# A one-core mixer layer: its first block loaded and multiplied in halves, a dot product ahead of an addition, and one split ahead of a norm

## Chip, core and metric

The kernel runs on one core of a Trainium2 chip. The metric is the device time of one execution in microseconds (us). The engines are named as in the profile: PE (TensorE, with PEld for its weight loads), DVE (VectorE), ACT (ScalarE), POOL (GpSimd), and SP (SyncE), which issues the transfers.

## What is computed

One layer of a hybrid backbone: the reference, cut to what the first stage of the kernel works on, is

```python
x = x + sincos_2d(n_lat, 1024)                       # x: 1024 tokens x 1024 channels
mod_lat = silu(c) @ ada_w + ada_b                    # 3 x 1024: shift, scale, gate
sh, sc, gt = split(mod_lat, 3)
h = rms_norm(x, norm_g) * (1 + sc) + sh
z = h @ w_in                                         # 56 column blocks of 128
u_lru, z_lru, u_fft, z_fft, u_pool, z_pool, gates = split(z)
# three branches (RG-LRU scan, Fourier mixing, pooling), each gated by silu(z_*),
# projected, merged by sigmoid gates, multiplied by w_out, added to x, normed
```

The context tokens go through the same weights later and only serve the scan's first states.

## The kernel before

Everything is kept transposed: channels on the 128 partitions, tokens along the row. `x` is eight tiles `xt[k]` of 128x1024, a block of `w_in` is 128 channels by 8 k by 128 columns. Products are made of parts: every float32 operand is split into a rounded high part and a rest (`split`: the high part is an ACT cast, the low part a DVE subtraction), and three products (high high, low high, high low) are added in PSUM.

The first stage makes the eight blocks z0 to z7 of `z_lru` before and around the norm. The norm needs the sum of squares over all channels, so z0 to z5 are multiplied with `x` scaled per channel only (`xs`: high part `xh`, rest `xl`), and the result is multiplied with the tokens' `rstd` afterwards; the shift is put in as a bias. The scale per channel, `gsc`, is a dot product of a row of the ada weights with silu(c): `dot_scale(k, 0)` on DVE, from the tile `ada_t[8 + k]` and `sb[0]`.

Loop over k = 0 to 7 (the loop around `dot_scale(k, 0)` and `wave(k, chunk(k, FIRST), xs)` in the listing): `dot_scale`, `xs_hi` (ACT), the square of `xt[k]` (ACT), `add_pos(k + 1)` (the positional term, DVE), `squares_add` (DVE), `xs_lo` (DVE), every second k the split of the next weight chunk, then `wave(k, ...)`: 24 products of 512 columns on PE, four blocks (z0 to z3) by three parts by two halves of the tokens. A chunk `wc` holds two k of the four blocks. In wave 7 the blocks come one after another (z2, z0, z1, then the sum of squares `ss` through a product with ones, then z3); ACT copies z0 to z2 out of PSUM (`copy_out`), z3 is read by DVE. Two ACT logarithms and two exponentials make `rstd` (`rstd_part`). Then eight waves of 12 products make z4 and z5 from the same `xs` (weights `wz`, two whole blocks), and eight more make z6 and z7 from the normed `ht` (high part `hh`).

All four engines other than PE issue in exactly the order of the code in this stage (`manual_schedule`), as PE does in the whole kernel; an engine that waits holds up all that stands behind it. SP issues transfers in code order too; a load waits until its buffer is free and until the eighth transfer before it has landed. Ahead of the first wave stands `warm_up(16)`, 16 calls of a float32 product (two products each on PE) on a constant tile.

Of the kernel before, what the change touches and what calls it, by code (L numbers as in the profile page):

```python
# [10 lines left out]
ALU = mybir.AluOpType  # L11
# [4 lines left out]
NK = 8  # L16
# [8 lines left out]
B_ULRU, B_ZLRU, B_UF, B_ZF, B_UP, B_ZP, B_G = 0, 8, 16, 20, 24, 28, 32  # L25
# [3 lines left out]
def tile_hybrid_mixer(  # L29
# [26 lines left out]
    V, S, G, PE, SP = nc.vector, nc.scalar, nc.gpsimd, nc.tensor, nc.sync  # L56
# [11 lines left out]
    def f4(name, shape=(128, 1024), pool=None):  # L68
        return (pool or p4).tile(list(shape), F32, tag="t4", name=name)

    def f2(name, shape=(128, 512)):
        return p2.tile(list(shape), F32, tag="t2", name=name)

    def r4(name, shape=(128, 1024), pool=None):
        return (pool or p4).tile(list(shape), F32R, tag="t4", name=name)
# [4 lines left out]
    def acc(name):  # L80
        return pacc.tile([128, 1024], F32, tag="acc", name=name)
# [28 lines left out]
    def f(t):  # L110
        return t.bitcast(F32)

    def act(o, i, func=AF.Identity, **kw):
        S.activation(out=o, in_=i, func=func, **kw)  # L114

    def tt(o, a, b, op):
        V.tensor_tensor(o, a, b, op=op)  # L117

    def stt(o, a, s, b, op0, op1, **kw):
        V.scalar_tensor_tensor(o, a, s, b, op0=op0, op1=op1, **kw)  # L120
# [15 lines left out]
    class Weight:  # L136
        def __init__(self, name, src, shape=(128, NK, 128), pools=(praw, pwt, pwt)):
            self.name, self.shape, self.pools = name, shape, pools
            self.raw = f4(name + "_f", shape, pools[0])
            SP.dma_start(out=self.raw, in_=src)  # L140

        def mk(self):
            self.hi, self.lo = (r4(self.name + n, self.shape, p) for n, p in zip(("_h", "_l"), self.pools[1:]))
# [46 lines left out]
    def mm3(o, pairs, first=True, last=True):  # L190
        n = len(pairs)
        for i, (wh, wl, xh, xl) in enumerate(pairs):
# [5 lines left out]
    sml = const.tile([128, N_SMALL], F32, name="sml")  # L198
    pos = const.tile([128, 320], F32, name="pos")
# [6 lines left out]
    gsc, shc = ([[const.tile([128, 1], F32, name=f"{n}{v}_{k}") for k in range(NK)] for v in range(2)]  # L206
                for n in ("gsc", "shc"))
# [23 lines left out]
    def item(key):  # L231
        for pre, b in (("u", B_ULRU), ("z", B_ZLRU), ("UF", B_UF), ("ZF", B_ZF), ("UP", B_UP), ("ZP", B_ZP),
                       ("g", B_G), ("h", B_G + 8), ("i", B_G + 16)):
            if key[:-1] == pre:
                return key, in_block(b + int(key[-1])), KK
        n = int(key[-1])
        return key, {"pa": pa, "pb": pb, "pc": pc}[key[:-1]][n], KK
# [4 lines left out]
    with tc.manual_schedule(engines={ET.PE}):  # L242
# [17 lines left out]
        xt = [f4(f"x{k}") for k in range(NK)]  # L260
        sb = [f4("sb0"), None]
        ada_t, wt, cx = {}, {}, []
        H = [slice(0, HALF), slice(HALF, T)]

        def load_ada(n):
            ada_t[n] = f4(f"ada{n}")
            SP.dma_start(out=ada_t[n], in_=ada[n])
# [3 lines left out]
        chunks = []  # L271

        def load_chunk(c):
            chunks.append(Weight(f"wc{c}", w_in[B_ZLRU:B_ZLRU + 4, :, 2 * c:2 * c + 2, :].rearrange("b p k o -> p b k o"),
                                 (128, 4, 2, 128), CHUNK_POOLS[c]))

        CHUNK_POOLS = ((praw, pwt, pwt),) * 3 + ((praw, p4, p4),)

        def load_w(nm):
            wt[nm] = Weight("w" + nm, item(nm)[1], KK, (praw, p4, p4))  # L280

        SP.dma_start(out=sb[0], in_=cc[0:1, :].to_broadcast([128, 1024]))
        load_ada(8)
        for k in range(NK):
            SP.dma_start(out=xt[k], in_=xT[k])
            if k == 0:
                SP.dma_start(out=pos, in_=k_pos)
                SP.dma_start(out=sml, in_=small)
            else:
                load_ada(8 + k)  # L290
            if k in (0, 2, 4):
                load_chunk(k // 2)
        SP.dma_start(out=edge, in_=k_edge)

        def add_pos(k, eng=V):
            v = xt[k].rearrange("p (r c) -> p r c", c=64)
            if k < 4:
                e = pos[:, k * 16:(k + 1) * 16].unsqueeze(2).to_broadcast([128, 16, 64])
            else:
                e = pos[:, 64 + (k - 4) * 64:64 + (k - 3) * 64].unsqueeze(1).to_broadcast([128, 16, 64])  # L300
            eng.tensor_tensor(v, v, e, op=ALU.add)
# [6 lines left out]
        def warm_up(n):  # L308
            for _ in range(n):
                PE.matmul(out=pre_ps[:, 0:512], lhsT=warm[:, 0:128], rhs=warm, start=True, stop=True)  # L310


        def rstd_part(vs, pss):
            for v, ps in zip(vs, pss):
                act(v, ps, AF.Ln, scale=1.0 / D, bias=eps)
            for v in vs:
                act(v, v, AF.Exp, scale=-0.5)


        def dot(t, v, dst):  # L320
            stt(junk, t, 1.0, sb[v], ALU.mult, ALU.mult, accum_out=dst)

        def dot_scale(k, v):
            t = ada_t.pop(8 + k)
            g = gsc[v][k]
            dot(t, v, g)
            stt(g, g, b1[:, k:k + 1], sml[:, O_NG + k:O_NG + k + 1], ALU.add, ALU.mult)

        def dot_shift(k, v):
            s_ = shc[v][k]  # L330
            dot(ada_t.pop(k), v, s_)
            tt(s_, s_, sml[:, O_AB + k:O_AB + k + 1], ALU.add)


        xs = {}

        def xs_hi(k):
            xs[k] = r4(f"xh{k}"), r4(f"xl{k}")
            act(xs[k][0], xt[k], scale=gsc[0][k])

        def xs_lo(k):
            stt(xs[k][1], xt[k], gsc[0][k], f(xs[k][0]), ALU.mult, ALU.subtract)
# [11 lines left out]

        def wave(k, ws, src):
            for n in range(3):
                for nm, hi, lo in ws:
                    o = pacc_t[nm]
                    for h in range(2):
                        x = src[k][n == 2][:, H[h]]  # L360
                        PE.matmul(out=bank(o, h), lhsT=lo if n == 1 else hi, rhs=x,  # L361
                                  start=k == 0 and n == 0, stop=k == NK - 1 and n == 2)

        def chunk(k, names):
            w = chunks[k // 2]
            return [(nm, w.hi[:, b, k % 2, :], w.lo[:, b, k % 2, :]) for b, nm in enumerate(FIRST) if nm in names]
# [4 lines left out]
        def bank(o, h):  # L371
            return o[h] if isinstance(o, list) else o[:, H[h]]
# [22 lines left out]

        act(sb[0], sb[0], AF.Silu)
        V.tensor_scalar(b1, sml[:, O_AB + 8:O_AB + 16], 1.0, 0.0, op0=ALU.add, op1=ALU.add)
        warm_up(16)
        sqs, zv = None, {}
        pacc_t = {"z0": acc("z0"), "z1": acc("z1"), "z2": acc("z2"), "z3": acc("z3")}  # L400


        def copy_out(nm):
            zv[nm] = [f2(f"v{nm}_{h}") for h in range(2)]
            o = pacc_t.pop(nm)
            for h in range(2):
                S.copy(zv[nm][h], bank(o, h))
# [14 lines left out]
        def squares_add(k):  # L422
            if k:
                tt(sq[0], sq[0], sq[k], ALU.add)
                del sq[k]


        add_pos(0)
        for k in range(NK):
            dot_scale(k, 0)  # L430
            if k == 0:
                chunks[0].ready()
            xs_hi(k)
            sq[k] = f4(f"sq{k}")
            act(sq[k], xt[k], AF.Square)
            if k < NK - 1:
                add_pos(k + 1)
            if k:
                squares_add(k - 1)
            xs_lo(k)  # L440
            if k % 2 and k < NK - 1:
                chunks[k // 2 + 1].ready()
            if k == 0:
                load_chunk(3)
            if k == 3:
                load_w("z4")
            if k == 4:
                load_w("z5")
            if 1 < k < 6:
                load_ada(k - 2)  # L450
            if k < NK - 1:
                wave(k, chunk(k, FIRST), xs)
        act(rss[:, 0:1], eps, AF.Ln)
        wt["z4"].ready()
        wave(7, chunk(7, ["z2"]), xs)
        copy_out("z2")
        wave(7, chunk(7, ["z0"]), xs)
        wave(7, chunk(7, ["z1"]), xs)
        ps = acc("ss")
        ps = [ps[:, sl] for sl in H]  # L460
        squares_add(7)
        for h in range(2):
            PE.matmul(out=ps[h], lhsT=ones, rhs=sq[0][:, H[h]], start=True, stop=True)
        sq.clear()
        copy_out("z0")
        rstd_part([rstd[:, H[0]], rstd[:, H[1]]], ps)
        copy_out("z1")
        wave(7, chunk(7, ["z3"]), xs)
        dot_shift(0, 0)
        load_ada(4)  # L470
        dot_shift(1, 0)
        load_ada(5)
        wt["z5"].ready()
        dot_shift(2, 0)
        load_ada(6)
        dot_shift(3, 0)
# [907 lines left out]
```

## Time and profile before

| | us |
|---|---|
| median of 3 runs | 1002.89 (1002.65 to 1003.63) |
| the profiled execution | 1002.09 |
| its span, first to last instruction | 1000.3 |
| PE busy in it | 988.7 |
| DVE busy | 582.1 |
| ACT busy | 522.2 |

The profile shows one execution. Times in it count from the start of the span. A group of instructions bears the line of the code that recorded it, which can be that of a helper (L114 is `act`, L117 `tt`, L120 `stt`, L129 the cast and L134 the subtraction of `split`, L361 the product of `wave`); so tiles tell more than lines. Buffer numbers are left out of names: `xh` is any `xh` of the eight, told apart by their times. A bracket at the end of a row tells how long the engine was idle ahead of it and what released it.

### The profile page before, as it was taken

What the parts mean: (1) busy time and instruction counts of PE and PEld (TensorE: products, weight loads), DVE (VectorE), ACT (ScalarE), POOL (GpSimd) and SP (SyncE); (2) the same over time, 40 slices, a digit from 0 to 9 for tenths busy, and PEclk for the clock granted to TensorE, in tenths of its full rate; (3) what the DMA queues carried; (4) which work ended last, traced back from release to release, by engine and by line L of the source; (5) the groups of instructions that cost most, each with busy time, mean ns of one, the idle gap of its engine ahead of it and who ended that gap; (6) DMA issues with size and microseconds to landing.
All of it is one profiled execution on the core that took longest, in us unless ns stands there. A gap on an engine that the chain in (4) does not pass through costs nothing.

```text
span 1000.3 us, 11785 instructions
## 1 busy us (share of the span) xinstructions
PE 988.7 (99%) x4686; PEld 810.3 (81%) x4686; DVE 582.1 (58%) x746; ACT 522.2 (52%) x618; POOL 21.7 (2%) x22
## 2 busy tenths in 40 slices
PE   9989999999999999999999999999999999999997
PEld 5868788878788887888878888778888888888886
DVE  6959457538557485563845628256565674456063
ACT  4443464295793956939599394884332221213131
POOL 0000000000000000000000000000000000000341
PEclk9999999999999999999999999999999999999999
DMA  9532595131322222343243312357655785324272
GB/s 347 229 108 83 197 382 231 64 105 67 108 103 96 101 85 90 127 166 134 70 167 105 132 64 95 106 184 258 217 185 187 244 315 188 137 91 134 71 252 75
DMA packets 48838, 152.53 MB, mean 152 GB/s; under 512 B 6544, under 2 KB 10128, under 8 KB 48784
## 3 DMA queue, kind: packets, MB, share of 16 engines
q1 hardware_dynamic: 48640, 151.53, 43.0%
q8 instruction: 37, 0.61, 0.2%
q10 hardware_dynamic: 144, 0.26, 0.1%
q14 instruction: 17, 0.14, 0.0%
HBM read 114.01 MB, written 37.75 MB: 152 GB/s over the span
## 4 chain that ended last, share of the span: by engine, by line
PE 94%; ACT 4%; DMA 1%; DVE 0%; issue 0%; POOL 0%; DVEq 0%; SPq 0%; POOLq 0%
PE z L361 9%; PE pi L193 3%; PE pg L193 3%; PE o L195 3%; PE pi L195 3%; PE o L193 3%; PE o L194 3%; PE pi L194 3%; PE pg L194 3%; PE ppa L195 3%; PE ppa L193 3%; PE pu L195 3%; PE pg L195 3%; PE pu L194 3%; PE pu L193 3%; PE ppa L194 3%
## 5 line engine op out<-in xcount | busy, mean ns | idle before, releaser
L114 ACT ACT_TABLE_LOAD x74 | 94.9, 1283 | 2.0 <-PEq L1374 0.7
L117 DVE TENSOR_TENSOR i<-i,xc 128x1024 f32<-128x1024 f32 x16 | 19.0, 1223 | 58.9 <-ACT i L114 58.9
L194 PE MATMUL o<-wo_l,mh 128*128 128x512 f32 (+1 forms) x136 | 51.2, 377 | 0.0
L195 PE MATMUL o<-wo_h,mh 128*128 128x512 f32 (+1 forms) x136 | 51.2, 376 | 0.0
L193 PE MATMUL o<-wo_h,ml 128*128 128x512 f32 (+1 forms) x136 | 51.2, 376 | 0.0
L193 PE MATMUL pi<-hh,i_l 128*128 128x512 f32 x128 | 50.8, 397 | 0.0
L193 PE MATMUL ph<-hh,h_l 128*128 128x512 f32 x128 | 50.5, 395 | 0.2
L193 PE MATMUL pg<-hh,g_l 128*128 128x512 f32 x128 | 50.5, 394 | 0.0
L194 PE MATMUL pi<-hl,i_h 128*128 128x512 f32 x128 | 49.9, 390 | 0.0
L195 PE MATMUL ph<-hh,h_h 128*128 128x512 f32 x128 | 49.9, 390 | 0.0
L195 PE MATMUL pi<-hh,i_h 128*128 128x512 f32 x128 | 49.9, 390 | 0.0
L194 PE MATMUL ph<-hl,h_h 128*128 128x512 f32 x128 | 49.8, 389 | 0.0
L194 PE MATMUL pg<-hl,g_h 128*128 128x512 f32 x128 | 49.8, 389 | 0.0
L195 PE MATMUL pg<-hh,g_h 128*128 128x512 f32 x128 | 49.8, 389 | 0.0
L193 PE MATMUL pu<-hh,u_l 128*128 128x512 f32 x128 | 49.8, 389 | 0.0
L194 PE MATMUL pu<-hl,u_h 128*128 128x512 f32 x128 | 49.8, 389 | 0.0
L195 PE MATMUL pu<-hh,u_h 128*128 128x512 f32 x128 | 49.8, 389 | 0.0
L193 PE MATMUL ppa<-yh,pa_l 128*128 128x512 f32 x128 | 49.8, 389 | 0.0
L194 PE MATMUL ppa<-yl,pa_h 128*128 128x512 f32 x128 | 49.8, 389 | 0.0
L195 PE MATMUL ppa<-yh,pa_h 128*128 128x512 f32 x128 | 49.8, 389 | 0.0
L129 ACT CAST xh<-xc 128x1024 fp32r<-128x1024 f32 x8 | 8.4, 1054 | 75.1 <-DVE xc L120 52.8
L120 DVE SCALAR_TENSOR_TENSOR junk<-ada,sb 128x1024 bf16<-128x1024 f32 x32 | 39.0, 1219 | 13.5 <-DMA ada<-in_ada 13.5
(378 smaller groups left out, 2614.8 us busy)
## 6 DMA issues: line engine op xcount, KB each, us to landing
ada<-in_ada SPq DMA_DIRECT2D x32, 512.0 KB, 8.6
x<-in_xT SPq DMA_DIRECT2D x8, 512.0 KB, 10.0
u_f<-in_w_in SPq DMA_DIRECT2D x8, 512.0 KB, 4.0
i_f<-in_w_in SPq DMA_DIRECT2D x8, 512.0 KB, 4.5
k_i<-ei SPq DMA_DIRECT2D x8, 512.0 KB, 2.9
z<-k_z SPq DMA_DIRECT2D x8, 512.0 KB, 5.4
k_y<-z SPq DMA_DIRECT2D x8, 512.0 KB, 2.6
h_f<-in_w_in SPq DMA_DIRECT2D x8, 512.0 KB, 4.3
```

What stands on the lines that cost most here:

```text
L114: S.activation(out=o, in_=i, func=func, **kw)
L117: V.tensor_tensor(o, a, b, op=op)
L120: V.scalar_tensor_tensor(o, a, s, b, op0=op0, op1=op1, **kw)
L129: S.copy(hi, src)
L193: PE.matmul(out=o, lhsT=wl, rhs=xh, start=first and i == 0, stop=False)
L194: PE.matmul(out=o, lhsT=wh, rhs=xl, start=False, stop=False)
L195: PE.matmul(out=o, lhsT=wh, rhs=xh, start=False, stop=last and i == n - 1)
L361: PE.matmul(out=bank(o, h), lhsT=lo if n == 1 else hi, rhs=x, start=k == 0 and n == 0, stop=k == NK - 1 and n == 2)
```

## The change

Three things are changed in the first stage.

- The first block. `x0` and the first weight chunk are loaded in halves: tokens 0 to 511, the chunk's first k, the other tokens, the second k. The small tables (`sml`, `pos`) come ahead of them, and each ada tile is loaded ahead of its `x` tile instead of behind it. `first_block()` runs `dot_scale(0, 0)` in front of the addition of the positional term, and adds, scales and splits in halves. `wave(0, ...)` takes the first halves of the tokens of all blocks first. `warm_up` makes 7 calls instead of 16.
- The dot product stands in front of the addition for this first k; for the others the order in code stays.
- In wave 7 the split of z5's weights (`wt["z5"].ready()`) and two of the shift products (`dot_shift`) stand in front of z1's product and so of the norm; z0 and z1 are copied out directly behind their products.

```diff
-            SP.dma_start(out=self.raw, in_=src)
+            if src is not None:
+                SP.dma_start(out=self.raw, in_=src)
...
+        SP.dma_start(out=sml, in_=small)
         load_ada(8)
-        for k in range(NK):
+        SP.dma_start(out=pos, in_=k_pos)
+        w0 = Weight("wc0", None, (128, 4, 2, 128), CHUNK_POOLS[0])
+        for h in range(2):
+            SP.dma_start(out=xt[0][:, H[h]], in_=xT[0][:, H[h]])
+            SP.dma_start(out=w0.raw[:, :, h, :],
+                         in_=w_in[B_ZLRU:B_ZLRU + 4, :, h, :].rearrange("b p o -> p b o"))
+        chunks.append(w0)
+        for k in range(1, NK):
+            load_ada(8 + k)
             SP.dma_start(out=xt[k], in_=xT[k])
...
-                for nm, hi, lo in ws:
-                    o = pacc_t[nm]
-                    for h in range(2):
+                order = [(w, h) for w in ws for h in range(2)]
+                if k == 0 and n == 0:
+                    order.sort(key=lambda v: v[1])
...
-        warm_up(16)
+        warm_up(7)
...
-        add_pos(0)
+        def first_block():
+            w = chunks[0]
+            w.mk()
+            dot_scale(0, 0)
+            x, e = xt[0].rearrange("p (r c) -> p r c", c=64), pos[:, 0:16].unsqueeze(2).to_broadcast([128, 16, 64])
+            xs[0] = r4("xh0"), r4("xl0")
+            S.copy(w.hi[:, :, 0, :], w.raw[:, :, 0, :])
+            for h in range(2):
+                r = slice(8 * h, 8 * h + 8)
+                tt(x[:, r], x[:, r], e[:, r], ALU.add)
+                act(xs[0][0][:, H[h]], xt[0][:, H[h]], scale=gsc[0][0])
+            S.copy(w.hi[:, :, 1, :], w.raw[:, :, 1, :])
+            for r in range(2):
+                tt(w.lo[:, :, r, :], w.raw[:, :, r, :], f(w.hi[:, :, r, :]), ALU.subtract)
+                if not r:
+                    xs_lo(0)
+            w.raw = None
+
+        first_block()
...
         wt["z4"].ready()
+        squares_add(7)
         wave(7, chunk(7, ["z2"]), xs)
         copy_out("z2")
         wave(7, chunk(7, ["z0"]), xs)
+        copy_out("z0")
+        for k in range(2):
+            dot_shift(k, 0)
+        wt["z5"].ready()
         wave(7, chunk(7, ["z1"]), xs)
+        copy_out("z1")
...
-        squares_add(7)
...
-        copy_out("z0")
...
-        copy_out("z1")
         wave(7, chunk(7, ["z3"]), xs)
-        dot_shift(0, 0)
         load_ada(4)
-        dot_shift(1, 0)
         load_ada(5)
-        wt["z5"].ready()
```

What this does to the order of the built programs is seen at three places. On SP, the first transfers of the program, before (`in_cc` is silu's argument, `in_small` the table `sml`, `in_ada` the ada weights, `in_xT` the tiles of x, `in_w_in` the weights):

```order
L282 DMA sb_133<-in_cc 128x1024
L267 DMA ada_135<-in_ada 128x1024
L285 DMA x_125<-in_xT 128x1024
L287 DMA pos<-in_k_pos 128x320
L288 DMA sml<-in_small 128x124
L140 DMA wc_f<-in_w_in 128x4x256
L285 DMA x_126<-in_xT 128x1024
L267 DMA ada_143<-in_ada 128x1024
```

The same place now:

```order
L284 DMA sb_133<-in_cc 128x1024
L285 DMA sml<-in_small 128x124
L268 DMA ada_136<-in_ada 128x1024
L287 DMA pos<-in_k_pos 128x320
L290 DMA x_125<-in_xT 128x512
L291 DMA wc_f<-in_w_in 128x4x128
L290 DMA x_125<-in_xT 128x512
L291 DMA wc_f<-in_w_in 128x4x128
L268 DMA ada_144<-in_ada 128x1024
L296 DMA x_126<-in_xT 128x1024
```

The tables moved ahead of the first ada tile, the first x tile and the first chunk come in alternating halves, and the second ada tile stands ahead of the second x tile (`x_126`).

On DVE, the start of the program before (`pos` marks the additions, `ada` the dot products):

```order
L397 TENSOR_SCALAR sc_83<-sml_78 128x8
L301 TENSOR_TENSOR x0_125<-x0_125,pos_79 128x1024
L120 SCALAR_TENSOR_TENSOR junk_169,gsc0_0_84<-ada8_135,sb0_133 128x1024
L120 SCALAR_TENSOR_TENSOR gsc0_0_84<-gsc0_0_84,sc_83,sml_78 128x1
L134 TENSOR_TENSOR wc0_l_198<-wc0_f_140,wc0_h_197 128x1024
L301 TENSOR_TENSOR x1_126<-x1_126,pos_79 128x1024
L120 SCALAR_TENSOR_TENSOR xl0_202<-x0_125,gsc0_0_84,xh0_201 128x1024
L120 SCALAR_TENSOR_TENSOR junk_169,gsc0_1_85<-ada9_143,sb0_133 128x1024
```

The same place now:

```order
L404 TENSOR_SCALAR sc_83<-sml_78 128x8
L120 SCALAR_TENSOR_TENSOR junk_171,gsc0_0_84<-ada8_136,sb0_133 128x1024
L120 SCALAR_TENSOR_TENSOR gsc0_0_84<-gsc0_0_84,sc_83,sml_78 128x1
L117 TENSOR_TENSOR x0_125<-x0_125,pos_79 128x512 x2
L117 TENSOR_TENSOR wc0_l_188<-wc0_f_139,wc0_h_187 128x4x128
L120 SCALAR_TENSOR_TENSOR xl0_192<-x0_125,gsc0_0_84,xh0_191 128x1024
L117 TENSOR_TENSOR wc0_l_188<-wc0_f_139,wc0_h_187 128x4x128
L307 TENSOR_TENSOR x1_126<-x1_126,pos_79 128x1024
L120 SCALAR_TENSOR_TENSOR junk_171,gsc0_1_85<-ada9_144,sb0_133 128x1024
```

The first dot product moved ahead of the first addition, and the addition for `x1` now stands behind all of the first block's work.

On ACT, from the split of z4's weights to the first part of the normed input (`hh0`), before:

```order
L129 CAST wz4_h_471<-wz4_f_321 128x1024
L407 COPY vz2_0_481<-z2_192 128x512
L407 COPY vz2_1_482<-z2_192 128x512
L407 COPY vz0_0_501<-z0_190 128x512
L407 COPY vz0_1_502<-z0_190 128x512
L114 ACTIVATE rstd_168<-ss_497,eps_82 128x512 x2
L114 ACT_TABLE_LOAD
L114 ACTIVATE rstd_168<-rstd_168 128x512 x2
L407 COPY vz1_0_509<-z1_191 128x512
L407 COPY vz1_1_510<-z1_191 128x512
L129 CAST wz5_h_527<-wz5_f_359 128x1024
```

The same place now:

```order
L129 CAST wz4_h_468<-wz4_f_318 128x1024
L414 COPY vz2_0_479<-z2_185 128x512
L414 COPY vz2_1_480<-z2_185 128x512
L414 COPY vz0_0_489<-z0_183 128x512
L414 COPY vz0_1_490<-z0_183 128x512
L129 CAST wz5_h_497<-wz5_f_356 128x1024
L414 COPY vz1_0_507<-z1_184 128x512
L414 COPY vz1_1_508<-z1_184 128x512
L114 ACTIVATE rstd_170<-ss_511,eps_82 128x512 x2
L114 ACT_TABLE_LOAD
L114 ACTIVATE rstd_170<-rstd_170 128x512 x2
```

The cast of z5's weights and the copies of z1 moved from behind `rstd` to in front of it. On DVE the order of the additions of squares, the shift products and the splits of z4 and z5 is the same in both programs.

## Rows read from the trace of the kernel before

**Rows 1.** The page, busy us of each engine, share of span.

```profile
PE 988.7 (99%) x4686; PEld 810.3 (81%) x4686; DVE 582.1 (58%) x746; ACT 522.2 (52%) x618; POOL 21.7 (2%) x22
```

**Rows 2.** Waits of PE, whole span: who, for whom, us, times, longest.

```profile
PE z L361 <- ACT wz_h L129: 3.9, 1, 3.9
...
PE p L193 <- DVE al L134: 0.3, 1, 0.3
```

**Rows 3.** Table of stretches: length, busy us and count by engine, PEclk, DMA, GB/s.

```profile
66.70:69.80 3.10, 3.08 (x7) 2.49 (x8) 3.06 (x5) 0.00 (x0) 0.00 (x0) 0.51 0.00 0
```

**Rows 4.** Order of time, PE: start, us, operation, out<-in, count, idle before.

```profile
1.31 15.77 PE L310 MATMUL warm<-warm 128*128 128x512 f32 x32 [1.31 <-POOL warm L257]
...
16.52 2.41 PE L361 MATMUL z<-xh,wc_h 128*128 128x512 f32 x8
...
22.39 1.98 PE L361 MATMUL z<-xh,wc_h 128*128 128x512 f32 x8
...
55.03 0.62 PE L361 MATMUL z<-xh,wc_h 128*128 128x512 f32 x2
...
59.12 1.88 PE L463 MATMUL ss<-sq,ones 128*128 128x512 f32 x4
...
62.22 0.62 PE L361 MATMUL z<-xh,wz_h 128*128 128x512 f32 x2
...
89.58 1.07 PE L361 MATMUL z<-hh,wz_h 128*128 128x512 f32 x4
```

**Rows 5.** Order of time, ACT: `xh` of k = 2, then around the norm.

```profile
22.12 1.15 ACT L114 ACTIVATE xh<-x,gsc 128x1024 fp32r<-128x1024 f32 x1 [2.69 <-DVE gsc L120]
...
52.24 1.04 ACT L129 CAST wz_h<-wz_f 128x1024 fp32r<-128x1024 f32 x1
...
56.59 1.08 ACT L407 COPY vz<-z 128x512 f32<-128x512 f32 x2 [3.31 <-PE z L361]
...
61.03 1.26 ACT L114 ACTIVATE rstd<-ss,eps 128x512 f32<-128x512 f32 x2 [2.01 <-PE ss L463]
...
63.61 1.15 ACT L114 ACTIVATE rstd<-rstd 128x512 f32<-128x512 f32 x2
```

**Rows 6.** Order of time, SP: issues of `sml`, first chunk, x1.

```profile
2.59 0.56 SPq L288 DMA_DIRECT2D sml<-in_small  x1
3.19 0.62 SPq L140 DMA_DIRECT2D wc_f<-in_w_in  x1
3.86 0.61 SPq L285 DMA_DIRECT2D x<-in_xT  x1
```

**Rows 7.** Transfers issued at these three times: KB, us from issue to landing.

```profile
sml<-in_small SPq DMA_DIRECT2D x1, 62.0 KB, 6.2
...
wc_f<-in_w_in SPq DMA_DIRECT2D x1, 512.0 KB, 7.1
...
x<-in_xT SPq DMA_DIRECT2D x1, 512.0 KB, 7.7
```

**Rows 8.** Order of time, DVE: k = 1, then around the norm, z7's weights.

```profile
14.88 1.22 DVE L120 SCALAR_TENSOR_TENSOR junk<-ada,sb 128x1024 bf16<-128x1024 f32 x1
...
16.27 1.22 DVE L301 TENSOR_TENSOR x<-x,pos 128x1024 f32<-128x1024 f32 x1
...
54.45 1.22 DVE L117 TENSOR_TENSOR sq<-sq,sq 128x1024 f32<-128x1024 f32 x1
55.59 1.22 DVE L120 SCALAR_TENSOR_TENSOR junk<-ada,sb 128x1024 bf16<-128x1024 f32 x1
...
56.93 1.22 DVE L120 SCALAR_TENSOR_TENSOR junk<-ada,sb 128x1024 bf16<-128x1024 f32 x1
...
66.70 1.23 DVE L134 TENSOR_TENSOR wz_l<-wz_f,wz_h 128x1024 fp32r<-128x1024 f32 x1 [8.35 <-ACT wz_h L129]
...
70.81 1.28 DVE L117 TENSOR_TENSOR vz<-z,rstd 128x512 f32<-128x512 f32 x2
...
87.09 1.22 DVE L134 TENSOR_TENSOR wz_l<-wz_f,wz_h 128x1024 fp32r<-128x1024 f32 x1
```

More of the change, by code (lines that the diff above doesn't have):

```diff
@@ L282, in tile_hybrid_mixer @@
         SP.dma_start(out=sb[0], in_=cc[0:1, :].to_broadcast([128, 1024]))
+        SP.dma_start(out=sml, in_=small)
         load_ada(8)
-        for k in range(NK):
-            SP.dma_start(out=xt[k], in_=xT[k])
[L286 to L291, printed above, removed]
+        SP.dma_start(out=pos, in_=k_pos)
[7 more added lines that the diff above has]
+            load_ada(8 + k)
+            SP.dma_start(out=xt[k], in_=xT[k])
+            if k in (2, 4):
                 load_chunk(k // 2)
@@ L356, in wave @@
             for n in range(3):
-                for nm, hi, lo in ws:
-                    o = pacc_t[nm]
-                    for h in range(2):
-                        x = src[k][n == 2][:, H[h]]
-                        PE.matmul(out=bank(o, h), lhsT=lo if n == 1 else hi, rhs=x,
-                                  start=k == 0 and n == 0, stop=k == NK - 1 and n == 2)
+                order = [(w, h) for w in ws for h in range(2)]
+                if k == 0 and n == 0:
+                    order.sort(key=lambda v: v[1])
+                for (nm, hi, lo), h in order:
+                    x = src[k][n == 2][:, H[h]]
+                    PE.matmul(out=bank(pacc_t[nm], h), lhsT=lo if n == 1 else hi, rhs=x,
+                              start=k == 0 and n == 0, stop=k == NK - 1 and n == 2)
         def chunk(k, names):
@@ L425, in squares_add @@
                 del sq[k]
-        add_pos(0)
+        def first_block():
[16 more added lines that the diff above has]
+        first_block()
         for k in range(NK):
[L430 to L433, printed above, removed]
+            if k:
+                dot_scale(k, 0)
+                xs_hi(k)
             sq[k] = f4(f"sq{k}")
@@ L439, in tile_hybrid_mixer @@
                 squares_add(k - 1)
-            xs_lo(k)
+            if k:
+                xs_lo(k)
             if k % 2 and k < NK - 1:
```

## The prediction

> **What bounds the kernel now.** I read the page first: TensorE (PE) is busy for 988.7 of 1000.3 us [rows 1], so the time is its products plus what stands ahead of the first one, what it waits later, and what it does at a low clock. The waits of PE come next: from the first product on there is one long one, 3.9 us for `wz_h`, the high half of the sixth block's weights (z5), and one of 0.3 us far behind [rows 2]. The table of stretches adds to the long wait: behind it PE worked for 3.1 us at a granted clock of 0.51, so at 1.2 instead of 2.4 GHz [rows 3]. Then the order of time on PE: 16 warm-up calls (32 products) keep it until 16.5 us, and after that it runs without a hole through seven waves. A wave of 24 products takes (55.03 - 22.39) / 6 = 5.44 us, so a product takes 0.227 us and a wave of 12 takes 2.72 [rows 4]. Last I read DVE and ACT, which make the inputs of those waves. There the reader sees what the total hides: DVE's work for one k takes as long as a wave, and since PE starts late, `xh` of k = 2 is ready at 22.12 + 1.15 = 23.27 [rows 5] where PE wants it at about 27.8.
>
> So PE can't gain the whole 6 us between its possible start and 16.5. It overtakes DVE after about 4.5 us, and from there on only an earlier DVE helps.
>
> **The first block in halves.** What counts is the landing of x1, since DVE's chain goes on from there. Pieces land in the order of issue: `sml` at 2.59 + 6.2 = 8.79, the weight chunk at 3.19 + 7.1 = 10.29, x1 at 3.86 + 7.7 = 11.56 [rows 6, 7]. A 512 KB piece of x therefore takes 1.27 us of the queue, and a 512 KB chunk, whose rows in memory are 1 KB and not 4 KB, takes 1.50. With halves, rows of the chunk are 512 B. Quartering a row's length has cost 0.23 us; halving it again I put at 0.1 to 0.25 for both halves together, so one half takes about 0.85. Its bounds are 0.75 (half of a whole one; shorter rows give no reason for less) and 1.50 (as many rows as the whole chunk had). One ada tile now lands ahead of x1. So x1 lands at 11.56 + 1.27 + (2 x 0.85 - 1.50) = 13.0, and going back from there the second weight half lands at 10.5, the second x half at 9.6, the first weight half at 9.0.
>
> The Trainium skill, page "DMA: Bandwidth & Descriptors", section Bandwidth, speaks against this step: transfers are to be batched to 1 MiB or more, with 341 GB/s measured at 1 MB and 138 at 64 KB. The rows here show 512 KB in each 1.27 us, 413 GB/s, where pieces queue behind each other, so the trace doesn't agree for whole pieces; for halves no run here shows it yet. By 341 GB/s the four halves would take 3.1 us instead of my 3.0 and the sum would lose 0.1; what the rule would do at its worst is a rival below.
>
> DVE's and ACT's halves are cheap: two ACT copies of 128x512 take 1.08 us together [rows 5] and two DVE products of that size 1.28 [rows 8], against 1.04 and 1.22 for whole tiles. On ACT: cast of the first weight half 9.0 to 9.55, first half of `xh` to 10.15. There PE starts; its seven warm-up calls are 14 of 32 products and over by about 9. On DVE, the dot product goes first and hides under the landing of x0. The second addition ends at 10.3, the second half of `xh` at 10.95, `xl` at 12.25, the second low weight half at 12.9. The addition for x1 waits for its landing until 13.1, the dot product follows 1.14 later at 14.25, and the addition for x2 another 16.27 - 14.88 = 1.39 later, at 15.63. Before, it began at 16.27 [rows 8]. **DVE's chain so moves ahead by 0.64 us.** By the bounds of a weight half it is +0.75 (then DVE's own work is the limit, not x1) to -0.65.
>
> On PE: wave 0 from 10.15 to 15.6; wave 1 waits for `xh` of k = 1 until 16.9 and ends at 22.3; wave 2 waits for 23.27 - 0.64 = 22.65. Waves follow each other at 5.44, as DVE's k do, so wave 7 begins at 22.65 + 5 x 5.44 = 49.85 and PE stands at `ss` 59.12 - 55.03 = 4.09 later, at 53.95. `ss` needs the sum of squares, which DVE ends at 54.45 + 1.22 = 55.67 before and 55.03 now. **PE waits 1.1 us there, and `ss` begins at 55.1 instead of 59.12: 4.0 us gained.** This wait covers about 1 us of any mishap in the waves ahead of it.
>
> **The sixth block's split ahead of the norm.** DVE's order stays; ACT's changes. Wave z4/z5 begins 62.22 - 4.0 = 58.2. ACT ends `wz_h` of z4 at 53.28 - 0.64 = 52.65; then copies of z2 and z0 (1.08 each), the cast for z5 (1.04), ending at 55.85, and the copy of z1, to 56.9. Queued behind that is the logarithm for `rstd`, on which `ss` releases ACT 61.03 - 59.12 = 1.91 after its start, at 57.0: the moved cast costs it nothing, by 0.1 us. On DVE two shift products (56.93 - 55.59 = 1.34 each) fill the time from 54.95 to 57.65, then the low half for z5 ends at 58.85. PE reads it with the seventh product, at 58.2 + 6 x 0.227 = 59.55: 0.7 us to spare. **So the stall goes whole.** Eight waves take 21.76 us instead of 89.58 - 62.22 = 27.36: 5.6 gained, 3.9 of waiting and 1.7 of low clock.
>
> What is late next? `rstd` is ready at 57.0 + (63.61 + 1.15 - 61.03) = 60.75. DVE gets to the product for z3 at 57.65 + (70.81 - 66.70) = 61.75, so 9.05 earlier, and the transfers that SP holds back for DVE and PE there (ada 6 and 7, weights z6 and z7) move with it. The low weights of z7 are then ready at 87.09 + 1.22 - 9.05 = 79.25 [rows 8], and PE reads them at 58.2 + 21.76 + 1.36 = 81.3: 2 us to spare. Behind this stage both programs wait for the same things, so the rest moves as a whole.
>
> **The sum** is 4.0 + 5.6 = 9.6 us. The profiled execution took 1002.09 us (span 1000.3), which gives 992.5; the median of the runs, 1002.89, lies 0.8 above it and gives 993.3, which I predict.
>
> **Rivals.**
> 1. A new gap turns the clock down once, likeliest at `ss` (1.1 us idle). Price as after the old stall, 1.7 us: 995.0. Against it: 0.3 us of waiting at `p` left the clock alone [rows 2]; gaps between 0.3 and 3.9 the trace doesn't show. In waves 0 and 1 most of it would be hidden by the later waits. 8%.
> 2. Halves land no sooner than whole pieces did (1.27 and 1.50 each): x1 lands 2.6 us later than I take it, and DVE is 1.9 late instead of 0.64 early. All else kept, the time is 995.9. For it: a weight half has as many rows as a whole chunk. Against it: bytes set the pace of all pieces in [rows 6, 7]. This is the rule of "DMA: Bandwidth & Descriptors" in the Trainium skill at its worst. 7%.
> 3. The split for z5 does not do what it says: ACT or DVE come to it late, or z7's weights stall the next wave. If the whole 5.6 stays, 998.9. It needs an error of 2 us in the slack of 0.7 or 2. 6%.
> 4. Slower: the gap after seven warm-up calls (9 to 10.15) or the one before wave 1 drops the clock, and it stays at 1.2 GHz. A wave then takes 5.44 more, and 2.7 us of later waits hide the first half wave. The gain is gone and 2 us more when this lasts 2.6 waves; through all seven it gives 993.3 + 38.1 - 2.7 = 1028.7. Against it: after the old stall the low stretch lasted 3.1 us of dense work [rows 3]. 3%. That activity releases the clock is also what the Trainium skill says, "TensorE: Matmul & The Clock Gate", Part 1, and the trace agrees at 66.7.
>
> That nothing changes by more than 2 us either way needs 3 twice, or a piece of 4: 2%.
>
> **How the numbers follow.** My forecast has 74%. Its own bounds are 993.2 (a weight half of 0.75) and 994.6 (of 1.50). Below them I allow 1.2 us: the three runs of before lie 1.0 apart (1002.65 to 1003.63), and the first landings may come a little sooner in one run than in another. Above, the range goes 1 us on and takes rival 1 in. So 992.0 to 995.6; left out are 2, 3 and 4, and the 2% below: 18%. Faster by over 0.2% (2 us, about what a measurement tells from no change): 74 + 8 + 7 + 6 = 95%; within 2%; slower 3%.
>
> **What would show it.** Right: first z product near 10.2, `xh` of k = 2 begins near 21.5, wave 7 near 49.9, a wait of about 1 us at `ss` released by DVE's addition of squares, no wait for `wz_h`, a granted clock of 1.00 throughout, and the first z6 product near 80. Wrong: `ss` near 54 without a wait (DVE was earlier), x1 landing after 14, a clock under 1 before 60 us, or a wait in front of z5 or z7.

## The result, and the profile after

The changed kernel takes 992.49 us (median of 4 runs, 991.95 to 993.12), the kernel before 1002.77 beside it (1002.47 to 1003.63): a ratio of 0.9896, interval 0.9879 to 0.9913, so 10.3 us (8.7 to 12.1) less. The forecast was 993.3. The profiled execution took 992.99 us, its span is 991.1.

The page of the changed kernel, busy us of each engine, and its waits of PE (who, for whom, us, times, longest), beside [rows 1, 2]:

```profile
PE 980.3 (99%) x4668; PEld 805.6 (81%) x4668; DVE 582.2 (59%) x748; ACT 522.2 (53%) x620; POOL 21.8 (2%) x22
...
PE z L368 <- ACT xh L114: 2.3, 2, 1.4
PE warm L316 <- POOL warm L258: 1.3, 1, 1.3
PE ss L493 <- DVE sq L117: 0.9, 1, 0.9
```

The long wait for `wz_h` is gone. Three shorter ones stand earlier: two for `xh`, one at `ss`. The table of stretches (length, busy us and count by engine, PEclk, DMA, GB/s) shows the full clock in waves 1 to 7 and in the waves of z4 and z5, where [rows 3] had 0.51:

```profile
17.30:55.40 38.10, 37.31 (x162) 30.16 (x162) 35.10 (x42) 21.18 (x24) 0.00 (x0) 1.00 0.60 233
58.70:80.40 21.70, 21.70 (x97) 17.97 (x96) 21.13 (x40) 9.28 (x11) 0.00 (x0) 1.00 0.54 190
```

The order of time on PE in the changed kernel (start, us, operation, tiles, count, idle before), beside [rows 4]:

```profile
1.31 7.85 PE L316 MATMUL warm<-warm 128*128 128x512 f32 x14 [1.31 <-POOL warm L258]
10.57 2.17 PE L368 MATMUL z<-xh,wc_h 128*128 128x512 f32 x8 [1.42 <-ACT xh L114]
...
17.27 2.11 PE L368 MATMUL z<-xh,wc_h 128*128 128x512 f32 x8 [0.88 <-ACT xh L114]
...
23.00 2.12 PE L368 MATMUL z<-xh,wc_h 128*128 128x512 f32 x8
...
50.37 0.62 PE L368 MATMUL z<-xh,wc_h 128*128 128x512 f32 x2
...
55.47 1.95 PE L493 MATMUL ss<-sq,ones 128*128 128x512 f32 x4 [0.86 <-DVE sq L117]
...
58.65 1.07 PE L368 MATMUL z<-xh,wz_h 128*128 128x512 f32 x4
59.56 1.07 PE L368 MATMUL z<-xh,wz_l 128*128 128x512 f32 x4
```

PE starts 5.95 us sooner (10.57 against 16.52) but is only 3.65 ahead at `ss`, as it now waits for ACT and DVE. The waves of z4 and z5 take 80.41 - 58.65 = 21.76 us instead of 27.36, and the first z6 product stands at 80.41 instead of 89.58: 9.17 us ahead, as much as the span (9.2).

ACT and DVE around the norm in the changed kernel, beside [rows 5, 8]:

```profile
54.74 1.07 ACT L129 CAST wz_h<-wz_f 128x1024 fp32r<-128x1024 f32 x1
55.69 1.10 ACT L414 COPY vz<-z 128x512 f32<-128x512 f32 x2
57.46 1.27 ACT L114 ACTIVATE rstd<-ss,eps 128x512 f32<-128x512 f32 x2 [0.67 <-PE ss L493]
...
13.40 1.22 DVE L307 TENSOR_TENSOR x<-x,pos 128x1024 f32<-128x1024 f32 x1
...
15.98 1.22 DVE L307 TENSOR_TENSOR x<-x,pos 128x1024 f32<-128x1024 f32 x1
...
52.96 1.22 DVE L134 TENSOR_TENSOR wz_l<-wz_f,wz_h 128x1024 fp32r<-128x1024 f32 x1 [2.10 <-ACT wz_h L129]
54.11 1.22 DVE L117 TENSOR_TENSOR sq<-sq,sq 128x1024 f32<-128x1024 f32 x1
...
57.92 1.23 DVE L134 TENSOR_TENSOR wz_l<-wz_f,wz_h 128x1024 fp32r<-128x1024 f32 x1
...
78.88 1.22 DVE L134 TENSOR_TENSOR wz_l<-wz_f,wz_h 128x1024 fp32r<-128x1024 f32 x1
```

z5's low weights are done at 57.92 + 1.23 = 59.15. PE reads them with the third of the four products that begin at 59.56, so at 60.0 (a product takes 0.227 us). ACT still idles 0.67 us ahead of the logarithm: the cast moved in front of it costs it nothing. z7's low weights are ready at 80.10 and read at about 81.8.

### The profile page after: what moved, and what is told of

Read it like the earlier page. It is cut to its first block, busy times and chain, and to the rows that moved or that the text cites. A ratio compares the mean times of both kernels' runs of the same rounds, so it can differ in the third digit from the quotient of the medians.

```text
span 991.1 us, 11759 instructions
## 1 busy us (share of the span) xinstructions
PE 980.3 (99%) x4668; PEld 805.6 (81%) x4668; DVE 582.2 (59%) x748; ACT 522.2 (53%) x620; POOL 21.8 (2%) x22
## 3 DMA queue, kind: packets, MB, share of 16 engines
q1 hardware_dynamic: 49312, 151.53, 43.1%
## 4 chain that ended last, share of the span: by engine, by line
PE 89%; ACT 4%; DVE 2%; DMA 1%; issue 0%; DVEq 0%; SPq 0%
PE z L368 5%; PE pi L194 3%; PE pg L194 3%; PE o L195 3%; PE o L196 3%; PE pi L196 3%; PE pg L196 3%; PE o L194 3%; PE pi L195 3%; PE ppa L196 3%; PE ppa L195 3%; PE pu L194 3%; PE pg L195 3%; PE pu L196 3%; PE pu L195 3%; PE ppa L194 3%
```

## Experiments

Landings differ from execution to execution: the addition of `pos` to x2 begins between 15.78 and 16.45 us in programs that load alike. So the table gives for each kernel the median of its runs and, from the order of time on PE in one profiled execution, the first z product, `ss`, the distance between them, and the first z6 product.

| kernel | median us | first z | ss | distance | z6 |
|---|---|---|---|---|---|
| before | 1002.77 | 16.52 | 59.12 | 42.60 | 89.58 |
| changed | 992.49 | 10.57 | 55.47 | 44.90 | 80.41 |
| again | 992.30 | 10.37 | 55.28 | 44.91 | 80.24 |
| part_a | 998.99 | 10.40 | 55.30 | 44.90 | 86.27 |
| part_b | 997.28 | 16.58 | 59.20 | 42.62 | 84.08 |
| warm11 | 999.01 | 12.46 | 55.55 | 43.09 | 86.28 |
| simple | 993.33 | 12.72 | 55.79 | 43.07 | 80.71 |
| gap3 | 993.33 | 11.02 | 55.93 | 44.91 | 80.87 |
| tables | 992.17 | 10.32 | 55.22 | 44.90 | 80.16 |
| gsq | 1000.83 | 10.71 | 63.37 | 52.66 | 88.33 |
| swap | 992.49 | 10.99 | 55.34 | 44.35 | 80.31 |
| sqfirst | 991.77 | 10.59 | 54.51 | 43.92 | 79.40 |
| gsq7 | 991.58 | 10.86 | 54.82 | 43.96 | 79.71 |
| best | 991.00 | 10.27 | 53.83 | 43.56 | 78.72 |

**The whole change again, and each part alone.** `again` is the changed kernel; `part_a` has the first block in halves and 7 warm-up calls, without the new order around the norm; `part_b` has that order alone:

```diff
         wt["z4"].ready()
+        squares_add(7)
...
+        copy_out("z0")
+        for k in range(2):
+            dot_shift(k, 0)
+        wt["z5"].ready()
```

> The changed kernel once more, beside the parts, with more rounds. Its profile put the gain at 9.2 us (the first z6 product at 80.41 instead of 89.58), the medians put it at 10.3. Theory 1 (the gain lies all ahead of z6 and the medians' surplus is run-to-run spread): 9.2 to 9.6 us faster. Theory 2 (something behind the first stage moved as well, so that the profiled execution shows too little): 10 to 10.5 us faster.

> The first block in halves, seven warm-up calls and the new order of the first transfers, with the order around the norm as before. Theory 1 (DVE's chain sets when the sum of squares is ready, and the old stall follows the norm): ss at 55.5, a wait of about 4 us for z5's high weights with a low clock behind it, 3.6 us faster than before. Theory 2 (an earlier start of PE counts by itself): 16.5 - 10.6 = 5.9 us faster.

> Only the order around the norm is changed: z5's split ahead of it. Theory 1: the wait of 3.9 us and the low clock behind it go whole, 5.6 us faster, and with the other part the gains add up to 9.2. Theory 2 (part of the stall comes back at z5's low weights or at z7's): less than 5, and the parts don't add up.

Measured: `again` 0.9898 [0.9883, 0.9913], 10.5 us; `part_a` 0.9961 [0.9948, 0.9973], 3.8 us; `part_b` 0.9946 [0.9934, 0.9959], 5.5 us. In the profiles `part_a` is 3.3 us ahead at z6 and `part_b` 5.5; together 8.8, the whole change 9.2 to 9.3. (By the medians `again` gained what its second theory expected, by the marks what the first did. From z6 to the end of the span its profile takes 990.5 - 80.24 = 910.3 us, the kernel before 910.7, where PE waits for `al` [rows 2]. But the changed kernel's own profile takes 910.7 as well (its weight loads wait 0.35 for the same `al`), so this half microsecond differs between executions of one program and isn't shown to be the change's.) Waits of PE, `part_a`:

```profile
PE z L368 <- ACT wz_h L129: 4.1, 1, 4.1
PE z L368 <- ACT xh L114: 1.6, 2, 0.9
PE warm L316 <- POOL warm L258: 1.3, 1, 1.3
PE ss L488 <- DVE sq L117: 0.9, 1, 0.9
```

and its stretch behind the first of them:

```profile
63.60:67.00 3.40, 3.40 (x10) 2.63 (x9) 3.30 (x9) 0.00 (x0) 0.00 (x0) 0.50 0.21 48
```

The stall of 4 us and the low clock behind it belong to the order around the norm alone, and the 5.6 us of that step is confirmed. In the profiles the parts add up to the whole within half a microsecond; the medians leave 1.0 to 1.2, which their intervals (1.2 us each way) cover.

**Is it the halves, or only fewer warm-up calls?** `warm11` is the kernel before with one number changed, and `simple` is `part_b` with the same number:

```diff
-        warm_up(16)
+        warm_up(11)
```

> The kernel before with 11 warm-up calls instead of 16 and nothing else: PE is free at about 12.6, when the whole first block is ready (12.7). Theory 1 (what held PE were the warm-up calls, and what holds it now is DVE's chain, so halves bring only the 0.3 us by which DVE's chain is earlier): ss at 55.8, 3.3 us faster than before, all but 0.3 of what the whole first part brings. Theory 2 (the halves' earlier start matters): about 2 us less than the first part, so 1.5 us faster.

> The kernel before with 11 warm-up calls and the order around the norm, but with x0 and the first weights whole and in the old order of loads. T1 (halves bring nothing beyond the earlier start of PE): ss near 55.5 as with 11 warm-up calls alone, no stall for the sixth block's weights, first z6 product near 80.5, and the time within 0.5 us of the changed kernel: 992.3 to 992.8. T2 (the halves move DVE's chain by the 0.64 us of the prediction): ss near 55.9, z6 near 81.0, 993.0 to 993.6.

`warm11` measured 0.9964 [0.9952, 0.9977], 3.75 us, as much as `part_a`, and at z6 both stand 3.3 us ahead. PE's first z product follows the warm-up calls at 12.46 without a wait; at `ss` PE waits for the same addition of squares as the changed kernel:

```profile
PE z L361 <- ACT wz_h L129: 3.9, 1, 3.9
PE warm L310 <- POOL warm L257: 1.3, 1, 1.3
PE ss L463 <- DVE sq L117: 0.4, 1, 0.4
```

`simple` measured 0.9907 [0.9893, 0.9920], 9.5 us. At z6 it stands 0.3 to 0.5 us behind the changed kernel, by the medians 0.8 to 1.0. So warm-up calls had held PE up, and cutting five of them gives nearly all of the first part. The halves let PE start 2.1 us sooner still, but the distance to `ss` grows from 43.1 to 44.9 in return; 0.3 to 0.5 us is left in the profiles. The medians would allow twice that, and which of the two holds is open. Whatever it is, it belongs to the halves, the new order of loads and the dot product's place together; no run parts them.

**What does a low clock in wave 0 cost?** `gap3` is the changed kernel with 3 warm-up calls:

```diff
-        warm_up(7)
+        warm_up(3)
```

> The changed kernel with 3 warm-up calls (6 products) instead of 7, so that PE stands idle from about 5 to 10.4 us. T1 (the waits ahead of wave 1, wave 2 and ss, 0.88 + 0.41 + 0.86 us in the changed kernel, are a reserve that hides what a low clock in wave 0 costs): a stretch at the low clock of about 3.4 us, as behind the old 3.9 us stall, makes wave 0 about 1.7 us longer; wave 1 then begins near 18.0 instead of 17.27, the waits shrink, ss begins within 0.3 us of 55.4, and the time is 992.3 within 0.5. T2 (the low clock is paid in full, or lasts): ss near 57 or later, 994.0 or more.

Measured: 0.9906 [0.9892, 0.9919], 9.5 us. The order of time on PE and DVE, and the table of stretches:

```profile
1.31 5.11 PE L316 MATMUL warm<-warm 128*128 128x512 f32 x6 [1.31 <-POOL warm L258]
11.02 3.78 PE L368 MATMUL z<-xh,wc_h 128*128 128x512 f32 x8 [4.60 <-ACT xh L114]
14.60 2.73 PE L368 MATMUL z<-xh,wc_l 128*128 128x512 f32 x8
...
19.01 1.98 PE L368 MATMUL z<-xh,wc_h 128*128 128x512 f32 x8
...
51.65 0.62 PE L368 MATMUL z<-xh,wc_h 128*128 128x512 f32 x2
...
54.56 1.22 DVE L117 TENSOR_TENSOR sq<-sq,sq 128x1024 f32<-128x1024 f32 x1
...
55.93 1.96 PE L493 MATMUL ss<-sq,ones 128*128 128x512 f32 x4
...
9.40:16.10 6.70, 5.08 (x12) 4.06 (x13) 5.91 (x7) 3.44 (x5) 0.00 (x0) 0.50 1.05 391
16.20:55.00 38.80, 38.80 (x172) 32.10 (x172) 35.73 (x45) 21.37 (x23) 0.00 (x0) 1.00 0.64 246
```

Behind 4.6 us of idle time the clock is at 0.50 until 16.1, and wave 0 takes 19.01 - 11.02 = 7.99 us instead of 17.27 - 0.88 - 10.57 = 5.82, so some 2.2 more. Yet `ss` stands 44.91 behind the first product, as in the changed kernel, because the waits shrink. By the marks, wave 0 and the wait behind it take 7.99 for 6.70, 1.29 more; from wave 7 to `ss` it is 55.93 - 51.65 = 4.28 for 55.47 - 50.37 = 5.10, 0.82 less; and waves 1 and 2, which PE now runs without a wait, make up the rest. (The 0.41 that was expected there is idle time of PE's weight loads for `xh`, not of its products.) Here too `ss` comes 0.15 behind DVE's addition of squares (54.56 + 1.22 = 55.78), so the reserve was just enough. `ss` came 0.5 later than was expected, with the first z product 0.45 late: this execution's first ada tile landed that much later. The median, 993.33, is 0.8 to 1.0 above the changed kernel's and outside the range of the first theory; the intervals cover that. So the marks of one profile show that waits on the way to `ss` are a reserve; that the low clock costs nothing in the median is not shown.

**Does sml in front cost anything?** `tables` moves the small table behind the first ada tile:

```diff
-        SP.dma_start(out=sml, in_=small)
         load_ada(8)
+        SP.dma_start(out=sml, in_=small)
```

> The changed kernel with sml (the small table) issued behind the first ada tile instead of ahead of it, so that the first ada tile and what follows it land about 0.3 us earlier. T1 (x1's landing, 13.38 in the changed kernel, sets DVE's chain): x1 lands near 13.1, ss begins 0.3 earlier (55.1) and the time is 0.3 lower, 992.0. T2 (x1's landing is set by all the bytes ahead of it, whatever their order, or DVE's own work in the first block is the limit): no movement within 0.1 us.

Measured: 0.9896 [0.9881, 0.9911], 992.17. `ss` begins 0.25 sooner than in the changed kernel and 0.06 sooner than in `again`. That agrees with a cost of up to 0.3 us, but is no more than executions differ. The other profiles point the same way: x1 lands at 13.13 here and at 13.09 in `best`, where the small table stands behind, and at 13.18 to 13.84 in the eight profiles with halves where it stands ahead. The size stays open.

**Is DVE's chain the bound, and can POOL relieve it?** `gsq` gives POOL six of the seven additions of squares, `gsq7` only the last one:

```diff
-                tt(sq[0], sq[0], sq[k], ALU.add)
+                (V if k == 7 else G).tensor_tensor(sq[0], sq[0], sq[k], op=ALU.add)
```

(in `gsq7` the other way round: G for k = 7.)

> The changed kernel with the additions of squares of k = 1 to 6 on POOL (GpSimd), the last one still on DVE. T1 (DVE's chain sets when ss may begin: 0.86 us of waiting for the addition of squares): DVE gets 1.14 us shorter for each k from k = 2 on, PE runs from wave 2 (23.0) without a wait, ss begins at 54.5 instead of 55.4 and the time is 0.9 lower, 991.4. POOL needs about 2.6 us for one addition (two halves of 1.30 in the program's rows on POOL) of 5.44 for each k. T2 (POOL's additions slow DVE's own, since both read the same memory): DVE's operations of 1.22 get longer while POOL works, ss begins at 55.4 or later, time 992.3 or more.

> The changed kernel with only the last addition of squares on POOL. It tells why the six additions on POOL cost 8.5 us. T1 (POOL and DVE exclude each other: whoever has begun an operation on two tensors holds the other up until it ends, as DVE's 1.22 became 2.74 and 3.42 there): POOL's 2.5 us fall into DVE's idle time from 50.9 on, DVE's split of z4's weights is held up until about 53.4 and ends 0.4 to 0.5 later than in the changed kernel, ss begins without a wait at 54.6, time 0.86 lower: 991.5. T2 (POOL as such is late or its release is slow): ss later than 55.4, time 992.3 or more.

`gsq` measured 1000.83, 0.998 [0.9971, 0.9988]: 8.3 to 8.5 us are lost of 10.3. DVE and POOL in the order of time:

```profile
18.39 2.55 POOL L431 TENSOR_TENSOR sq<-sq,sq 128x1024 f32<-128x1024 f32 x1 [16.99 <-ACT sq L114]
25.70 2.47 POOL L431 TENSOR_TENSOR sq<-sq,sq 128x1024 f32<-128x1024 f32 x1 [4.76 <-ACT sq L114]
...
19.28 2.74 DVE L134 TENSOR_TENSOR wc_l<-wc_f,wc_h 128x1024 fp32r<-128x1024 f32 x1 [0.61 <-ACT wc_h L129]
...
25.84 3.42 DVE L120 SCALAR_TENSOR_TENSOR junk<-ada,sb 128x1024 bf16<-128x1024 f32 x1
```

The dot product that begins at 25.84, while POOL's addition runs (25.70 to 28.17), ends at 29.26: 1.1 after POOL's, nearly its whole own length. So does the split: it ends at 22.02, and POOL's addition at 20.94. In both DVE stands still until POOL is done: it loses 1.5 and 2.2 us in two k where it saves 2 x 1.14. It also idles 0.61 ahead of each split, waiting for ACT or for the weights; in the changed kernel the additions fill this time for k = 3 and 5. That makes 2.0 of the 2.5 us by which two k got longer (38.00 - 24.65 = 13.35 between waves 2 and 4 for 2 x 5.44); the other 0.5 is not accounted for. This is the rule of the Trainium skill, "SBUF — State Buffer", section "Who interferes with whom", that DVE and GpSimd share one port pair and that it is an exclusive lock; the trace agrees, with 2.74 and 3.42 us for 1.22. In `gsq7` the one addition falls into DVE's idle time:

```profile
50.87 2.55 POOL L431 TENSOR_TENSOR sq<-sq,sq 128x1024 f32<-128x1024 f32 x1 [49.47 <-ACT sq L114]
...
53.28 1.23 DVE L134 TENSOR_TENSOR wz_l<-wz_f,wz_h 128x1024 fp32r<-128x1024 f32 x1 [2.12 <-ACT wz_h L129]
```

and the time is 991.58, 0.9886 [0.9869, 0.9902]. The distance from first z to `ss` is 0.94 shorter than in the changed kernel: the wait at `ss` is gone. DVE's split was not held up, against what was expected, since it waited for ACT's cast until POOL was as good as done.

**The same by order alone.** `sqfirst` puts the last addition of squares in front of z4's split on DVE, `swap` the cast of the second chunk in front of the square of x1 on ACT, and `best` has both and the order of loads of `tables`:

```diff
-        wt["z4"].ready()
         squares_add(7)
+        wt["z4"].ready()
```

```diff
-            act(sq[k], xt[k], AF.Square)
+            if k != 1:
+                act(sq[k], xt[k], AF.Square)
...
                 chunks[k // 2 + 1].ready()
+            if k == 1:
+                act(sq[k], xt[k], AF.Square)
```

> The changed kernel with the last addition of squares in front of the split of z4's weights on DVE, where DVE stands idle for 2.1 us (from 50.87) waiting for ACT's cast. T1 (the wait of 0.86 us at ss is only this one addition's place in DVE's order): the addition ends near 52.1, z4's low weights stay where they are, ss begins behind z1's last product at 54.6 without a wait and the time is 0.86 lower than the changed kernel's: 991.5. T2 (something else is late next: rstd, since ACT's copies end near 56.8, or z5's low weights): ss earlier, but z6 gains less than 0.5.

> The changed kernel with ACT's cast of the second weight chunk in front of its square of x1, so that DVE's 0.6 us of idle time at 19 us goes. T1 (DVE's chain sets both the wait ahead of wave 2 and the one at ss): the addition for x3 and all of DVE's later work move 0.6 ahead, the wait ahead of wave 2 (0.41) goes, ss still waits for DVE and begins 0.6 earlier (near 54.8), and the time is 0.6 lower: 991.8. T2 (the transfers of x3 or of its ada tile, which land at 15.96 and 14.66, or PE bound the chain there): less than 0.2.

> The changed kernel with three more changes together: the last addition of squares in front of z4's split, the cast of the second chunk in front of the square of x1, and sml issued behind the first ada tile. T1: 0.86 for the wait at ss, 0.41 for the wait ahead of wave 2 and 0.25 for the earlier landings: ss near 54.0, first z6 product near 78.9, 990.8. T2 (rstd or the weights of z6 and z7 are late next and take it back): 991.5 or more, with a new wait of PE between ss and z6.

`sqfirst`: 991.77, 0.9889 [0.9875, 0.9904]. DVE in the order of time, and PE at `ss`:

```profile
50.82 1.22 DVE L117 TENSOR_TENSOR sq<-sq,sq 128x1024 f32<-128x1024 f32 x1
53.02 1.23 DVE L134 TENSOR_TENSOR wz_l<-wz_f,wz_h 128x1024 fp32r<-128x1024 f32 x1 [0.98 <-ACT wz_h L129]
...
54.51 1.88 PE L493 MATMUL ss<-sq,ones 128*128 128x512 f32 x4
```

No wait is left at `ss`, and z6 stands 0.8 to 1.0 ahead of the changed kernel's two profiles. `swap`: the distance is 0.55 shorter, as its first theory says, but the median is 992.49, no lower: in its profile the first ada tile landed at 7.70 instead of 7.25, and whether that took the gain in the other runs too is open. `best`: 991.00 (990.62 to 991.49), 0.9882 [0.9867, 0.9897], the lowest median of all; z6 is at 78.72, 1.7 ahead of the changed kernel's. In its profile 0.4 us of that is lost again at `p`, where PE waits for DVE's `al` as it did for 0.3 us in [rows 2]. The intervals of `best` and of the changed kernel overlap; that it is faster rests on the marks and on run ranges (990.62 to 991.49 against 991.95 to 993.12) that don't touch, though the two were not measured side by side (the kernel before took 1002.62 beside `best` and 1002.77 beside the changed kernel).

## Why the prediction held, point by point

- **PE's start and what it gives back.** First z was put at 10.15 and came at 10.57; wave 1 at 16.9, came at 17.27; `xh` of k = 2 near 21.5, came at 21.79; wave 2 at 22.65, came at 23.00. PE does overtake DVE there, and `warm11` and `simple` show that a start earlier than 12.5 us brings no more than half a microsecond in the profiles.
- **Landings.** Of the terms, a weight half was right: put at 0.85, with bounds 0.75 and 1.50, and measured at 0.8 from the issues and the times to landing (here the first ada tile, the first weight half and x1):

```profile
1.65 0.42 SPq L268 DMA_DIRECT2D ada<-in_ada  x1
...
3.06 0.43 SPq L291 DMA_DIRECT2D wc_f<-in_w_in  x1
...
5.80 0.45 SPq L296 DMA_DIRECT2D x<-in_xT  x1
...
ada<-in_ada SPq DMA_DIRECT2D x1, 512.0 KB, 5.6
...
wc_f<-in_w_in SPq DMA_DIRECT2D x1, 256.0 KB, 6.2
...
x<-in_xT SPq DMA_DIRECT2D x1, 512.0 KB, 7.6
```

  So 256 KB with rows of 512 B land at 3.06 + 6.2 = 9.3 and the piece before them at 2.59 + 5.9 = 8.5. Rival 2 (halves that take as long as whole pieces) falls. x1 itself was put at 13.0 and landed at 5.80 + 7.6 = 13.4. The first ada tile came at 1.65 + 5.6 = 7.25 instead of 1.18 + 5.6 = 6.8. `sml`, now ahead of it, takes some 0.2 of that (it lands 0.18 behind the piece ahead of it), and the forecast had counted it among the pieces ahead of x1; the rest it had not, and `again`, with x1 at 13.18, shows how much of it differs from one execution to the next.
- **DVE's advance.** This is the mis-sized term: "0.64 us" became 16.27 - 15.98 = 0.29 (0.49 in `again`). x1's late landing explains it, since DVE's addition for x1 begins at 13.40, 0.02 behind it, and the one for x2 follows 2.58 later, where 15.63 - 13.1 = 2.53 was forecast.
- **The first part.** 4.0 us forecast, 59.12 - 55.47 = 3.65 measured, with a wait of 0.86 at `ss` where 1.1 was forecast, released by DVE's addition of squares as named. Wave 7 came at 50.37 for 49.85.
- **The second part.** 5.6 forecast, 27.36 - 21.76 = 5.60 measured, 5.5 alone. z5's low weights had 60.0 - 59.15 = 0.9 us to spare where 0.7 was forecast, z7's about 1.7 of the 2. ACT's cast for z6 now waits 0.78 us for its weights to land, and DVE 0.47 for the cast; PE sees nothing of it. Rival 3 falls.
- **The clock.** Idle times of 1.42, 0.88 and 0.86 us left it at 1.00, so rival 1 and rival 4 fall. `gap3` shows rival 4's premise, a gap that drops the clock, but the clock came back within wave 0, and its price there, some 2.2 us, went into the reserve in that profile, as that rival said of its first 2.7.
- **The sum.** 9.6 forecast, 9.2 in the profiles (9.3 in `again`), 10.3 and 10.5 by medians. The profiled execution of before lies 0.7 below its median and that of the changed kernel 0.5 above: that is the whole difference between 9.1 and 10.3. So the mechanism gave a little less than was worked out, and that the median still came out below the forecast is luck as far as the traces show: where a typical execution gains the further microsecond, no profile tells.

## What to carry to other kernels

When an engine is let start sooner, work out where it overtakes the engine that feeds it; from there on only that one's chain counts, and a cheap edit (a shorter warm-up) can give nearly as much as an elaborate one. Waits that are left on the way are a reserve that hides later mishaps, but the operation that ends the last one may simply stand behind another that idles: look for idle time just ahead of it on its own engine. Here, work moved from DVE to POOL paid only where DVE stood idle meanwhile.

## What the runs showed of the hardware

- DVE operations on two tensors that began while POOL was adding two tensors ended some 1.1 us behind POOL's: 1.22 us became 2.74 and 3.42 (`gsq`, six times of six).
- TensorE's clock was at 1.00 behind idle times of up to 1.5 us (`gsq`, 1.51 ahead of a wave), and at 0.50 or 0.51 behind 3.9, 4.1 and 4.6 us. It came back under dense work: after 3.1 us [rows 3] and some 3.4 us (`part_a`), after 5 us of work in `gap3`.
- Pieces in one queue landed in the order of issue. In the changed kernel 256 KB landed 0.7 us behind the piece ahead with rows of 2 KB, and 0.8 us behind it with rows of 512 B; whole 512 KB pieces took 1.27 [rows 6, 7].
